# A third gate tile in the stick-breaking list, and bias rows placed behind the gate stores

## The chip, the cores and the metric

The kernel runs on one core of one Trainium2 chip. The metric is the device time of one execution in microseconds (us); lower is better. Engines are named as in the profile: PE (matmul), ACT, DVE, POOL, and SP, which here only issues transfers. POOL issues transfers too.

## The reference

One layer of a hybrid streaming encoder, on a prompt of 1024 rows and a sample of 32 rows, model width 1024. Cut to what matters here:

```python
ada = silu(c) @ w_ada + b_ada            # 6 vectors of 1024: shift1, scale1, gate1, shift2, scale2, gate2
h   = rms_norm(x) * (1 + scale1) + shift1
p   = h @ w_in                           # q/kv latents, rope key, SB q, SB k, SB v, gate A, gate B
z   = einsum('bqhd,bshd->bhqs', q, k) * SB_SCALE            # branch B, stick-breaking, 8 heads
sp  = where(mask, softplus(z), 0)
a   = where(mask, exp(log_sigmoid(z) - (reverse_cumsum(sp) - sp)), 0)
o_B = einsum('bhqs,bshd->bqhd', a, v)
merged = sigmoid(gate_A) * (o_A @ w_proj_a) + sigmoid(gate_B) * (o_B @ w_proj_b)
x   = x + gate1 * rms_norm(merged @ w_out)                  # then the conv FFN
```

## The kernel before, in words

Every fp32 product is made of three matmuls on a high and a low part (`mm3`, L75 to L77). The stages follow one another: normalisation and the first two ada vectors, the q/k/v projection (to about 195 us), the stick-breaking attention (`stage_sb`, about 188 to 505 us), the latents, latent attention, merge, and the FFN.

`stage_sb` runs four passes, one per pair of heads. In each pass `sb_attend` walks a list written by hand, `ORDER`, whose tokens set the order of PE, ACT and DVE exactly. Tokens that matter here:

- `S` scores into a bank, `a e l E` steps on ACT, `x c k d` steps on DVE, `T` transposes (L805), `h v` their split, `V` products with the values, `o p` the output. `p` also stores it (`ob`, L955, on POOL's queue).
- `f` is one k-step (three matmuls) of the gate projection h @ w_in, which fills PE between attention steps. Eight steps make one block of 352 columns in a bank "mm"; there are two such banks.
- `G` empties a finished block: ACT copies the bank into a tile "nat" (L1078), and POOL stores the tile to DRAM (`gd`, L1079). There are two "nat" tiles, used in turn, so a copy waits for the store of the copy before last. PE may start a block only when its bank has been emptied.
- `W` and `w` split the next 128 columns of w_in (raw tile `wr`) into high and low on ACT and DVE.
- `A` multiplies four fetched tiles of w_ada (L240, 32 small matmuls into an "mm" bank), for the ada vectors v = 2 to 5: two `A` tokens in a pass, one vector in a pass. `D` adds the bank to the bias rows on DVE (L246), which frees the bank. For v > 2 the accumulator is one of two "ada" tiles, and `ada_bias` first fills it with the bias, broadcast over 32 partitions: four transfers on POOL's queue (L230).

PE, ACT and DVE obey the list. POOL and SP are placed by a scheduler that may bring a transfer forward when its tile is free. A POOL transfer also waits for the one eight places ahead of it, because eight completion semaphores take turns.

The tiles of `stage_sb` lie in one pool, placed by `place` and the lines around it in a fixed order.

Of the kernel before, what the change touches and what calls it, by code (L numbers as in the profile page):

```python
# [8 lines left out]
F32 = mybir.dt.float32  # L9
F32R = mybir.dt.float32r  # L10
# [7 lines left out]
P = 128  # L18
# [26 lines left out]
class K:  # L45
# [181 lines left out]
    def ada_bias(self, v):  # L227
        for j in range(4):
            c = v * D + j * 256
            self.nc.gpsimd.dma_start(self.acc[32 * j : 32 * j + 32], self.a["b_ada"][0, c : c + 256].partition_broadcast(32))  # L230

    def ada_step(self, n, pool, tp, late):

# [811 lines left out]
    def gates(self):  # L1045

        nc = self.nc
        v = lambda t: t.rearrange("p (k c) -> p k c", k=8)
        w, ps, ada = [self.w_in_tile(2208)], [], []
        self.next_w = w  # L1050
        raw = []

        def steps():
            for m in range(16):
                wh, wl = w.pop(0)
                for b, (c0, n) in enumerate(self.BLK):
                    if b == 0:
                        c = 2208 + (m + 1) * P if m < 15 else 3 * P
                        raw.append(self.wload([(0, 1024, self.a["w_in"][0, :, c : c + P].rearrange("(k p) c -> p k c", p=P), 8)]))
                    ps.append((m, c0, n, self.bank("mm")))  # L1060
                    for k in range(KT):
                        self.mm3(ps[-1][3][:, :n], wh[:, k], wl[:, k], self.Hh[k][:, c0 : c0 + n],
                                 self.Hl[k][:, c0 : c0 + n], k == 0, k == KT - 1)
                        if k < KT - 1:
                            yield
                    if b == 1 and self.ada_sum is not None:
                        ada.append(self.ada_turn())
                    yield

        step = steps()  # L1070

        def do(kind):
            if kind == "f":
                next(step)
            elif kind == "G":
                m, c0, n, x = ps.pop(0)
                g = self.tl(self.At, [P, 512], F32, "nat")
                nc.scalar.copy(g[:, :n], x[:, :n])  # L1078
                nc.gpsimd.dma_start(self.gd[m, :, c0 : c0 + n], g[:, :n])  # L1079
            elif kind == "A":  # L1080
                self.ada_step(4, self.sm2, self.Sp, ada)
                if not self.ada_todo:
                    self.sample_load(1)
            elif kind in "DQ":
                ada.pop(0)()
            elif kind == "W":
                w.append((self.tl(self.W, [P, 1024], F32R, "wh"), self.tl(self.W, [P, 1024], F32R, "wl")))
                self.hi(w[0][0], raw[0])
            else:
                self.lo(w[0][1], raw.pop(0), w[0][0])  # L1090
                w[0] = tuple(v(x) for x in w[0])

        return do
# [14 lines left out]
    def stage_sb(self):  # L1108
        nc = self.nc
        self.att_rows()  # L1110
        S = self.Sp = self.At = self.tc.alloc_tile_pool(name="sb", bufs=2, side="right", reuse_waits="tile")
        def place(*tags):
            for g, w in tags:
                for _ in range(2):
                    self.tl(S, [P, w], F32R if g[0] == "P" else F32, g)

        place(("o", 256), ("PTh", 512), ("PTl", 512))
        self.KLz, Q, KH, V = [None] * 2, [None] * 2, [None] * 2, [None] * 2
        t = lambda n: self.tl(S, [P, TP], F32R, n, 1)

        def values(p, h):
            if p:
                V[h] = t(f"V{h}")
            self.load(V[h].bitcast(F32).rearrange("r (t d) -> r t d", t=8), self.vd[p][:, :, h])

        def queries(p, h):
            r, o = slice(64 * h, 64 * h + 64), slice(64 - 64 * h, 128 - 64 * h)
            d = lambda x, n: self.load(x.bitcast(F32), self.spilt[n][p][r])
            if p:
                Q[h], KH[h] = t(f"Q{h}"), t(f"KH{h}")  # L1130
            d(Q[h][r], "qh")
            d(KH[h][r], "kh")
            d(KH[h][o], "kh")
            d(Q[h][o], "ql")
            d(self.KLz[h][r], "kl")
            d(self.KLz[h][o], "kl")

        V[1], self.KLz[1], Q[1], KH[1] = t("V1"), t("KL1"), t("Q1"), t("KH1")
        place(("ada", 256), ("nat", 512))
        self.diagonals(S)  # L1140
        for _ in range(3):
            self.tl(S, [P, TP], F32, "A")
        V[0], self.KLz[0], Q[0], KH[0] = t("V0"), t("KL0"), t("Q0"), t("KH0")
        self.sm2 = self.tc.alloc_tile_pool(name="att", bufs=2, reuse_waits="tile")
        for g, w, n in (("big", BIG, 3), ("A", TP, 2)):
            for _ in range(n):
                self.tl(self.sm2, [P, w], F32, g)

        self.sent = self.wlast
        queries(0, 0)  # L1150
        self.ada_w, self.ada_sum = [], None
        values(0, 0)

        def score(h, ps, i, c0, n):
            q = slice(i * P, (i + 1) * P)
            nc.tensor.matmul(ps[:, :n], Q[h][:, q], KH[h][:, c0 : c0 + n], start=True, stop=False)
            nc.tensor.matmul(ps[:, :n], Q[h][:, q], self.KLz[h][:, c0 : c0 + n], start=False, stop=True)

        fill = self.gates()
        E = mybir.EngineType  # L1160
        for p in range(4):
            then = {"S2.0a": lambda: queries(p, 1), "S2.1a": lambda: values(p, 1)}
            if p == 0:
                then["S2.1a"] = lambda: (values(p, 1), self.ada_fetch(4, self.sm2))
            if p < 3:
                then.update({"S3.1b": lambda: queries(p + 1, 0), "V3.0": lambda: values(p + 1, 0)})
            with self.tc.manual_schedule(engines={E.PE, E.Activation, E.DVE}):
                self.sb_attend(score, lambda b, h: V[h][:, b * P : b * P + P], self.store(self.obd[p]), fill, then)
        self.in_w.append(self.next_w.pop(0))
        S.release()  # L1170
        self.At = self.sm2
        self.sm3 = self.tc.alloc_tile_pool(name="att2", bufs=2, reuse_waits="tile")
# [1438 lines left out]
```

## Time and profile before

| | |
|---|---|
| median of 3 runs | 1694.51 us (1693.89 to 1695.26) |
| the profiled execution | 1695.23 us, of which the span is 1693.4 us |
| PE busy | 1650.3 us, 97% of the span |
| DVE / ACT / POOL busy | 1268.8 / 995.5 / 296.0 us |
| gate copies (L1078) | 48, the first at 199.2 us, the last at 502.6 us |
| gate stores (L1079) | 48, the first at 208.2 us, the last at 503.4 us |
| bias rows into "ada" (L230) | 12, the first at 201.2 us, the last at 344.0 us |

Timeline rows give: start, duration, engine, line and operation, output<-input, shape, count, and in brackets the idle time of that engine just before it and what ended it. A row of a wait gives: who waited, for whom, us in total, times, longest. Windows give busy time per engine, the TensorE clock that was granted (1.00 is full), the share of DMA engine time, and GB/s.

### The profile page before, as it was taken

The page shows a single profiled execution, that of the slowest core. Times are in us where ns is not written, and L with a number is a line of the kernel's source. Part 1 is how long each engine was busy: PE and PEld are TensorE (multiplying, and loading weights), DVE is VectorE, ACT ScalarE, POOL GpSimd, SP SyncE. Part 2 cuts the span into 40 slices and gives each one's busy share as a digit, 9 for nine tenths or more (in the row PEclk, how much of TensorE's full clock was granted, in tenths as well). Part 3 has the DMA queues.
Part 4 walks back from the last instruction along what each step waited for, and adds up shares of the span by engine and source line. Part 5 has one row for each costly group of instructions (what it writes and reads, how often), then busy time and mean ns, then how long its engine had stood idle before and what let it go on. Part 6 is the DMA issues. An engine that isn't in the chain of part 4 may idle for free. (4 is left out here: it accounts for less than half of the span.)

```text
span 1693.4 us, 30264 instructions
## 1 busy us (share of the span) xinstructions
PE 1650.3 (97%) x11646; PEld 1515.2 (89%) x11646; DVE 1268.8 (75%) x2121; ACT 995.5 (59%) x1945; POOL 296.0 (17%) x569
## 2 busy tenths in 40 slices
PE   5999999999999999999999999999999999999997
PEld 3999989999999898998888799999999999877885
DVE  4865778989883788877766789887787777787456
ACT  4544687878874577776762575444444444554442
POOL 3113312111110311110100222211111111200013
PEclk9999999999999999999999999999999999999999
DMA  9345875566631521221364532433333333697643
GB/s 336 104 133 178 286 232 161 161 190 181 178 116 47 152 65 51 69 82 50 130 228 137 181 115 85 152 105 132 129 102 129 130 104 123 239 323 247 206 141 121
DMA packets 185729, 255.22 MB, mean 151 GB/s; under 512 B 14702, under 2 KB 125056, under 8 KB 185584
## 3 DMA queue, kind: packets, MB, share of 16 engines
q1 hardware_dynamic: 164944, 194.11, 36.8%
q0 software_dynamic: 20416, 59.08, 10.0%
q8 instruction: 92, 1.51, 0.4%
q14 instruction: 53, 0.43, 0.1%
q10 hardware_dynamic: 224, 0.09, 0.0%
HBM read 187.86 MB, written 64.57 MB: 149 GB/s over the span
## 5 line engine op out<-in xcount | busy, mean ns | idle before, releaser
L68 ACT ACTIVATE wh<-wr 128x1024 fp32r<-128x1024 f32 (+5 forms) x163 | 132.1, 819 | 223.7 <-PE s L2065 82.2
L71 DVE TENSOR_TENSOR wl<-wr,wh 128x1024 fp32r<-128x1024 f32 (+5 forms) x163 | 150.2, 929 | 81.2 <-ACT wh L68 81.0
L75 PE MATMUL mm<-hh,wh 128*128 128x352 f32 x456 | 152.9, 335 | 3.7 <-ACT nat L1078 3.7
L76 PE MATMUL mm<-hl,wh 128*128 128x352 f32 x456 | 148.9, 326 | 0.1
L77 PE MATMUL mm<-hh,wl 128*128 128x352 f32 x456 | 148.6, 326 | 0.0
L2064 PE MATMUL mm<-T,wh 128*128 128x256 f32 (+1 forms) x376 | 108.1, 288 | 0.0
L2066 PE MATMUL mm<-T,wl 128*128 128x256 f32 (+1 forms) x376 | 107.1, 285 | 0.4 <-DVE wl L71 0.2
L2065 PE MATMUL mm<-T,wh 128*128 128x256 f32 (+1 forms) x376 | 106.6, 284 | 0.0
L2066 PE MATMUL s<-T,wl 128*128 128x256 f32 (+1 forms) x348 | 99.3, 285 | 0.0
L2064 PE MATMUL s<-T,wh 128*128 128x256 f32 (+1 forms) x348 | 99.2, 285 | 0.0
L2065 PE MATMUL s<-T,wh 128*128 128x256 f32 (+1 forms) x348 | 98.8, 284 | 0.0
L71 DVE TENSOR_TENSOR wl<-S,wh 128x1024 fp32r<-128x1024 f32 (+1 forms) x55 | 59.2, 1078 | 49.7 <-ACT wh L68 49.4
L75 PEld LDWEIGHTS mm<-hh,wh 128*128 128x128 f32 x456 | 86.7, 190 | 7.3 <-ACT nat L1078 3.9
L76 PEld LDWEIGHTS mm<-hl,wh 128*128 128x128 f32 x456 | 86.7, 190 | 2.8 <-issue 0.8
L2205 DVE SCALAR_TENSOR_TENSOR u<-u,c,u 128x1058 f32<-128x1058 f32 x68 | 87.0, 1317 | 2.0 <-ACT u L2202 0.7
L77 PEld LDWEIGHTS mm<-hh,wl 128*128 128x128 f32 x456 | 86.6, 190 | 0.2
L805 PE MATMUL tr<-c,A 128*128 128x128 f32 x576 | 85.0, 272 | 0.3 <-DVE A L921 0.3
L68 ACT ACTIVATE wh<-S 128x1024 fp32r<-128x1024 f32 (+1 forms) x55 | 51.8, 944 | 48.7 <-PE s L2065 13.4
L2064 PE MATMUL tr<-T,wh 128*128 128x272 f32 (+1 forms) x272 | 77.8, 286 | 0.0
L2066 PE MATMUL tr<-T,wl 128*128 128x272 f32 (+1 forms) x272 | 77.7, 286 | 0.0
L2065 PE MATMUL tr<-T,wh 128*128 128x272 f32 (+1 forms) x272 | 77.3, 284 | 0.0
L2195 POOL COPY c<-u 128x2 f32<-128x2 f32 x44 | 26.9, 611 | 265.9 <-DVE u L2141 229.9
(760 smaller groups left out, 5832.8 us busy)
## 6 DMA issues: line engine op xcount, KB each, us to landing
wr<-in_w_up_dram SPq DMA_DIRECT2D x44, 512.0 KB, 4.3
dr<-in_w_down_dram SPq DMA_DIRECT2D x43, 512.0 KB, 5.5
wr<-in_w_in_dram SPq DMA_DIRECT2D x33, 512.0 KB, 6.4
A<-in_w_ada_dram SPq DMA_DIRECT2D x32, 512.0 KB, 5.7
wr<-gdn SPq DMA_DIRECT2D x30, 512.0 KB, 4.2
gdn<-u POOLq DMA_DIRECT2D x23, 512.0 KB, 4.9
gd<-nat POOLq DMA_DIRECT2D x48, 176.0 KB, 3.5
t<-gd SPq DMA_DIRECT2D x16, 528.0 KB, 6.2
```

What stands on the lines that cost most here:

```text
L68: self.nc.scalar.activation(out, in_, AF.Identity, scale=scale)
L71: return self.nc.vector.tensor_tensor(out, full, hi.bitcast(F32), ALU.subtract)
L75: m(ps, lh, rh, start=start, stop=False)
L76: m(ps, lh, rl, start=False, stop=False)
L77: self.pe = m(ps, ll, rh, start=False, stop=stop).ins
L805: self.nc.tensor.transpose(tr[:, (2 * s + q) * P : (2 * s + q + 1) * P], at[q][:, b * P : b * P + P], self.idt)
L2064: m(ps[:, :n], w[0][:, k], x[0][:, k, c], start=first and k == 0, stop=False, skip_group_check=True)
L2065: m(ps[:, :n], w[0][:, k], x[1][:, k, c], start=False, stop=False, skip_group_check=True)
L2066: i = m(ps[:, :n], w[1][:, k], x[0][:, k, c], start=False, stop=k == 3, skip_group_check=True)
L2195: nc.gpsimd.tensor_copy(self.CV[:, 0:2, cc], u[:, 1024:1026])
L2205: nc.vector.scalar_tensor_tensor(y, u[:, w : w + YW], self.cvT[:, w, cc : cc + 1], y, ALU.mult, ALU.add)
```

## The change

Three edits. In the gate step the tile "nat" has three buffers while the list runs in the stick-breaking pool, and two in any other. `ada_bias` issues the rows of v > 2 only after the last gate store that the program has issued so far (`self.gsent`); that is an order on POOL's queue, not a wait for the store to land. `place` takes a count for each tag, so that the third tile has its place; the pool grows by 2 KB per partition, and the tiles placed after "nat" move by that much.

```diff
     def ada_bias(self, v):
         for j in range(4):
             c = v * D + j * 256
-            self.nc.gpsimd.dma_start(self.acc[32 * j : 32 * j + 32], self.a["b_ada"][0, c : c + 256].partition_broadcast(32))
+            with self.tc.issue_after(self.gsent) if v > 2 else ExitStack():
+                self.nc.gpsimd.dma_start(self.acc[32 * j : 32 * j + 32], self.a["b_ada"][0, c : c + 256].partition_broadcast(32))
...
             elif kind == "G":
                 m, c0, n, x = ps.pop(0)
-                g = self.tl(self.At, [P, 512], F32, "nat")
+                g = self.tl(self.At, [P, 512], F32, "nat", 3 if self.At is self.Sp else 2)
                 nc.scalar.copy(g[:, :n], x[:, :n])
-                nc.gpsimd.dma_start(self.gd[m, :, c0 : c0 + n], g[:, :n])
+                self.gsent = nc.gpsimd.dma_start(self.gd[m, :, c0 : c0 + n], g[:, :n]).ins
...
-        place(("o", 256), ("PTh", 512), ("PTl", 512))
+        place(("o", 256, 2), ("PTh", 512, 2), ("PTl", 512, 2))
...
-        place(("ada", 256), ("nat", 512))
+        place(("ada", 256, 2), ("nat", 512, 3))
```

The instructions of PE, ACT, DVE and SP stand in the same order in both programs. Only POOL's queue differs, in where twelve bias rows stand. Lines after L229 are one higher in the changed kernel (L1078 becomes L1079, L230 becomes L231).

POOL, at the start of the list's first pass, before the change. `sbd` is the last spill of the stage ahead, `ada` the bias rows of v = 3 and v = 4, `gd<-nat` the gate stores, `ob` an output store:

```order
L688 DMA sbd<-sb 32x512
L1105 MEMSET ptd_2210 128x128
L1105 MEMSET ptd_2211 128x128
L230 DMA ada_3552<-in_b_ada_dram 32x256 x4
L230 DMA ada_4544<-in_b_ada_dram 32x256 x4
L1079 DMA gd<-nat_2326 128x352
L1079 DMA gd<-nat_2365 128x352
L955 DMA ob_2181<-o_2435 64x256
```

The same place after the change:

```order
L689 DMA sbd<-sb 32x512
L1106 MEMSET ptd_2211 128x128
L1106 MEMSET ptd_2212 128x128
L1080 DMA gd<-nat_2327 128x352
L1080 DMA gd<-nat_2366 128x352
L956 DMA ob_2181<-o_2436 64x256
L1080 DMA gd<-nat_2475 128x352
```

The eight bias rows no longer stand ahead of the first two gate stores.

POOL, in the second pass, after the change; the rows of v = 3 stand here now, between the fourth and fifth gate store of the pass, shortly before the `A` token of the list:

```order
L1080 DMA gd<-nat_3325 128x352
L1080 DMA gd<-nat_3364 128x352
L956 DMA ob_2182<-o_3427 64x256
L1080 DMA gd<-nat_3466 128x352
L1080 DMA gd<-nat_3513 128x352
L231 DMA ada_3553<-in_b_ada_dram 32x256 x4
L956 DMA ob_2182<-o_3609 64x256
L1080 DMA gd<-nat_3622 128x352
```

The rows of v = 4 and v = 5 stand at the same place of the third and fourth pass; before the change those of v = 5 stood in the second pass, behind the store of `o_4041`.

More of the change, by code (lines that the diff above doesn't have):

```diff
@@ L1112, in place @@
         def place(*tags):
-            for g, w in tags:
-                for _ in range(2):
-                    self.tl(S, [P, w], F32R if g[0] == "P" else F32, g)
-        place(("o", 256), ("PTh", 512), ("PTl", 512))
+            for g, w, n in tags:
+                for _ in range(n):
+                    self.tl(S, [P, w], F32R if g[0] == "P" else F32, g, n)
+        place(("o", 256, 2), ("PTh", 512, 2), ("PTl", 512, 2))
         self.KLz, Q, KH, V = [None] * 2, [None] * 2, [None] * 2, [None] * 2
```

## The prediction

> **What bounds the kernel now.** The page's first part says which engine to follow:
>
> ```profile
> PE 1650.3 (97%) x11646; PEld 1515.2 (89%) x11646; DVE 1268.8 (75%) x2121; ACT 995.5 (59%) x1945; POOL 296.0 (17%) x569
> ```
>
> PE is busy 97% of the span, so an edit off PE's path pays only where PE stands still or runs slowly. I therefore read next who made PE wait, after the start-up:
>
> ```profile
> PE mm L75 <- ACT nat L1078: 3.7, 1, 3.7
> PE s L75 <- ACT mh L68: 1.8, 1, 1.8
> ```
>
> The longest stall is one wait for a gate copy, 3.7 us, once; the next is half of it and lies far behind this stage. The timeline of each engine shows where it comes from:
>
> ```profile
> 209.99 0.46 ACT L764 ACTIVATE A<-A 128x320 f32<-128x320 f32 x1
> 215.19 0.45 ACT L1078 COPY nat<-mm 128x352 f32<-128x352 f32 x1 [4.74 <-DMA gd<-nat]
> 215.70 0.43 PE L75 MATMUL mm<-hh,wh 128*128 128x352 f32 x1 [3.65 <-ACT nat L1078]
> 201.20 0.50 POOL L230 DMA_DIRECT2D ada<-in_b_ada_dram  x1 [1.58 <-DMA qh<-T]
> 206.75 1.48 POOL L230 DMA_DIRECT2D ada<-in_b_ada_dram  x3 [0.88 <-DMA ql<-fq]
> 208.22 1.12 POOL L1079 DMA_DIRECT2D gd<-nat  x2
> ```
>
> Read it backwards. PE waits 3.65 us for the third gate copy, which frees its bank. That copy stands 4.74 us on ACT, until the first gate store has landed and its "nat" tile is free. The first store was issued only at 208.22, behind eight bias rows that began at 201.20 and waited in between for spills ahead of them; it landed 215.19 - 208.22 = 7.0 us later.
>
> The windows around it show a second loss, the granted clock:
>
> ```profile
> 212.00:215.70 3.70, 0.05 (x2) 0.00 (x1) 0.37 (x1) 0.51 (x2) 0.00 (x0) 1.00 1.03 384
> 216.70:220.10 3.40, 3.40 (x13) 3.31 (x12) 2.62 (x5) 3.34 (x9) 0.54 (x1) 0.51 1.09 349
> ```
>
> After the stall PE runs 3.40 us at a granted clock of 0.51. What both cost is found without modelling either: the second pass walks the same list, so the same two instructions are taken before and behind the place, in the first pass and in the second:
>
> ```profile
> 205.26 0.49 ACT L744 ACTIVATE A<-s 128x384 f32<-128x384 f32 x1
> 287.26 0.49 ACT L744 ACTIVATE A<-s 128x384 f32<-128x384 f32 x1
> 225.05 0.41 DVE L246 TENSOR_TENSOR acc<-acc,mm 128x256 f32<-128x256 f32 x1
> 301.55 0.41 DVE L246 TENSOR_TENSOR ada<-ada,mm 128x256 f32<-128x256 f32 x1
> ```
>
> 287.26 - 205.26 = 82.00 us ahead of it, 301.55 - 225.05 = 76.50 us behind it. The first pass loses 5.50 us here: 3.65 idle and 1.85 of slow clock and restart.
>
> **The gate stores and the third tile.** Two edits attack the same wait. The third copy gets a tile of its own and waits for no store. The fourth takes the first tile again. Second-pass times less 82.00 give the undisturbed schedule:
>
> ```profile
> 294.93 0.45 ACT L1078 COPY nat<-mm 128x352 f32<-128x352 f32 x1
> L230 POOL DMA_DIRECT2D ada<-in_b_ada_dram x8: 498/498/502, 201.2 to 207.7; - x8
> DMA to landing us min/median/max: 4.9/6.1/6.6
> ```
>
> The fourth copy comes at 294.93 - 82.00 = 212.93. The first store now takes the queue place of the first bias row, 201.20; with the slowest of these landings, 6.6 us, it is in by 207.8, 5 us early. Should it take the 7.0 us measured later, 4.7 us are left. So the stall goes, and -5.50 us is the first term. Its bounds are 0 (something else holds the copy) and -5.50.
>
> **What is late next.** The 5.50 us covered two transfers that do not move with PE, because SP issued them before the stall:
>
> ```profile
> 222.00 1.93 PE L240 MATMUL mm<-A,cT 128*32 128x256 f32 x32
> L83 SPq DMA_DIRECT2D A<-in_w_ada_dram x1: 349/349/349, 206.7 to 206.7; - x1
> DMA to landing us min/median/max: 7.3/7.3/7.3
> 208.77 0.42 SPq L83 DMA_DIRECT2D wr<-in_w_in_dram  x1
> wr<-in_w_in_dram SPq DMA_DIRECT2D x1, 512.0 KB, 11.8
> DMA packets 129, 0.40 MB, mean 398 GB/s; under 512 B 10, under 2 KB 35, under 8 KB 129
> DMA packets 551, 0.33 MB, mean 331 GB/s; under 512 B 10, under 2 KB 536, under 8 KB 551
> 224.32 1.04 ACT L68 ACTIVATE wh<-wr 128x1024 fp32r<-128x1024 f32 x1
> ```
>
> The `A` step moves from 222.00 to 216.50 and needs its fourth w_ada tile after three quarters of 1.93 us, at 217.95. The first tile lands at 206.7 + 7.3 = 214.0, the `wr` load behind all four at 208.77 + 11.8 = 220.6. Spread evenly, the fourth lands at 214.0 + 3/4 x 6.6 = 218.9, a wait of 1.0 us. The packet rows (216 to 217 us, then 217 to 218) say sooner: the short packets of the `wr` load, 512 bytes a row, fill the second row, so the tiles ahead were nearly through by 217, plus about 1.2 us to land: 218.2, a wait of 0.3. It can't be later than the load behind it, 2.65 us, nor less than nothing. I take 0.4, near the packet rows. Then ACT's split of `wr` moves from 224.32 to 218.8 and waits up to 1.8 us for 220.6. What that costs PE is read from the slack behind the same step in the second pass:
>
> ```profile
> 304.63 0.69 DVE L762 TENSOR_TENSOR A<-s,A 128x512 f32<-128x512 f32 x1
> 306.85 0.33 PE L1156 MATMUL s<-KH,Q 128*128 128x384 f32 x1
> ```
>
> DVE frees the score bank at 305.32, PE wants it at 306.85: 1.53 us of slack. Of 1.8 - 0.4 = 1.4 us nothing, of 1.8 us 0.3 comes through; I take 0.1. Both together: +0.5, bounds 0 and 2.7.
>
> **The bias rows.** Twelve rows leave an early place and stand, four each, right behind the last gate store ahead of the `A` token of passes two to four. Nothing is added. POOL's own time is free: behind them stands an output store that waits for DVE anyway, idle 7.47 us. What may cost is that the `D` addition on DVE now waits for rows issued late, and behind it on DVE stands the rest of the list; PE's next gate block waits for the bank that `D` frees.
>
> ```profile
> 295.68 0.54 POOL L1079 DMA_DIRECT2D gd<-nat  x1 [2.02 <-ACT nat L1078]
> DMA to landing us min/median/max: 2.1/2.1/2.1
> 298.00:300.00 2.00, 2.00 (x33) 1.18 (x34) 2.00 (x4) 1.37 (x3) 0.00 (x0) 1.00 0.00 0
> 303.40 0.41 PE L75 MATMUL mm<-hh,wh 128*128 128x352 f32 x1
> 303.69 0.54 POOL L955 DMA_DIRECT2D ob<-o  x1 [7.47 <-DVE o L793]
> L230 POOL DMA_DIRECT2D ada<-in_b_ada_dram x4: 498/501/513, 342.5 to 344.0; - x4
> DMA to landing us min/median/max: 7.2/7.5/7.8
> ```
>
> The rows start at 296.22 and every 0.5 us after, the last at 297.72. The store just ahead landed in 2.1 us, and from 298 to 300 the queues move nothing, so the last row is in by about 299.9, ahead of `D` at 301.55 and of PE's need at 303.40. Cost 0. The far row is the last one: 7.8 us on full queues, landing at 305.5; `D` would wait 4.0 us, of which 303.40 - 301.96 = 1.44 are hidden, so 2.5 us in each of three passes, 7.6 us. I take 0, since the place is quiet.
>
> [...]
>
> **The moved tiles.** The pool's growth moves some waits between instructions. The farthest is a rope-key load in the next stage that now waits for stores of this list:
>
> ```profile
> L1278 SPq DMA_DIRECT2D nat<-in_cache_mla_krope_dram x2: 367/433/499, 539.2 to 539.6; - x2
> L1079 POOL DMA_DIRECT2D gd<-nat x48: 542/571/602, 208.2 to 503.4; - x48
> ```
>
> Some 36 us lie between; cost 0.
>
> **The sum.** -5.5 + 0.5 + 0 = -5.0 us. Against the profiled execution, 1695.23 us (span 1693.4), that gives 1690.2; against the median of 1694.51, which lies 0.7 lower, 1689.5. I take 1689.9. A measurement can tell some 0.2% from no change, 3.4 us, so "faster" begins below 1691.1.
>
> **The rivals.**
>
> *The w_ada tile takes the place of the store.* If the fourth tile lands as late as the load behind it, PE waits 2.65 us at `A` and the gain is 2.8: 1692.4 from the profiled time. For it: the queues are full from 200 to 220 us. Against it: the short packets from 217 on.
>
> *The slow clock isn't in the typical run.* Then the median holds only the 3.65 us of idling and some 0.2 of restart, and the gain is 3.85 - 0.5 = 3.35: 1691.2. For it: the profiled execution is 0.7 us above the median. Against it: the clock fell though PE had already worked 1 us again, so it needs no perfect alignment. [...]
>
> *Late bias rows: slower.* The one place is `D` in passes two to four. If a row needs L us to land, the loss is 3 x (L - 5.27), from 297.72 + L against 301.55 + 1.44. It beats the gain from L = 6.9; at 7.8 the sum is -5.0 + 7.6 = +2.6, 1697.8. For it: rows on full queues needed 7.2 to 7.8. Against it: the quiet window.
>
> *The change doesn't reach the stall*, because the third copy waits for something the trace can't show, such as what lay in the third tile's memory: 1694.5.
>
> **How the numbers follow.** Forecast 0.66, w_ada 0.12, clock 0.11, bias rows 0.06, no effect 0.05. Faster: the forecast and half of the clock case, 0.72. Same: w_ada, the other half, no effect, 0.22. Slower: 0.06. The range starts at the median less the whole 5.5 and 0.3 for the runs' own spread, 1688.7, and ends with the w_ada case, 1692.6; left out are the slow case and no effect.
>
> **What would show it.** Right: no idle before the third gate copy; the first store issued near 201; a granted clock of 1.00 from 212 to 221; the first `D` 5 us earlier; in passes two to four a `D` with no wait for a transfer. Wrong: a PE wait at the `A` step over 2 us, an ACT wait for `wr` that reaches PE, or a DVE wait before L247.

## The result, and the profile after

The changed kernel takes 1690.11 us (median of 22 runs, 1685.59 to 1692.03), the kernel before 1694.02 us (22 runs, 1689.95 to 1696.27). The ratio is 0.9978 with a 95% interval of 0.9972 to 0.9985, so it is 2.5 to 4.7 us faster, 3.7 us at the middle. The profiled execution has a span of 1687.8 us.

The stretch that held the stall, in the same windows as before (busy time of PE, its weight loads, DVE, ACT, POOL; granted clock; DMA share; GB/s):

```profile
PE 1650.3 (98%) x11646; PEld 1514.1 (90%) x11646; DVE 1268.5 (75%) x2121; ACT 995.0 (59%) x1945; POOL 294.9 (17%) x569
212.00:215.70 3.70, 3.70 (x25) 3.67 (x24) 3.44 (x6) 3.57 (x9) 1.11 (x2) 1.00 1.02 406
216.70:220.10 3.40, 3.19 (x40) 1.66 (x39) 3.04 (x7) 2.50 (x5) 0.00 (x0) 1.00 1.09 366
```

From 212.0 to 215.7 PE is busy throughout where it was idle, and from 216.7 the clock is 1.00 where it was 0.51. PE's busy time over the whole span is nevertheless the same to a tenth, 1650.3 us. The reason lies at the start of the program, where this execution ran at half clock for 3.4 us longer than the profiled execution before (first line: before; second: after):

```profile
32.44:35.85 3.41, 3.41 (x17) 1.86 (x17) 3.30 (x5) 2.07 (x4) 0.55 (x1) 0.50 1.05 384
32.46:39.29 6.83, 6.22 (x30) 3.32 (x31) 4.62 (x7) 4.91 (x7) 0.00 (x0) 0.50 1.05 387
```

The timelines of the engines concerned, after the change:

```profile
202.44 0.56 POOL L1080 DMA_DIRECT2D gd<-nat  x1 [1.73 <-ACT A L765]
211.32 0.45 ACT L1079 COPY nat<-mm 128x352 f32<-128x352 f32 x1
219.19 0.64 PE L241 MATMUL mm<-A,cT 128*32 128x256 f32 x8 [0.21 <-DMA A<-in_w_ada_dram]
221.05 1.06 ACT L68 ACTIVATE wh<-wr 128x1024 fp32r<-128x1024 f32 x1 [1.15 <-DMA wr<-in_w_in_dram]
```

The first gate store is issued at 202.44 (the list itself starts 1.0 us later in this execution), the third copy waits for nothing, and the two transfers that were to be late next are: 0.21 us of PE at the fourth w_ada tile, 1.15 us of ACT at the raw w_in tile. The pass offset, taken from the same score step in the first and second pass, and the same step to the first `D`:

```profile
206.23 0.49 ACT L745 ACTIVATE A<-s 128x384 f32<-128x384 f32 x1
220.53 0.41 DVE L247 TENSOR_TENSOR acc<-acc,mm 128x256 f32<-128x256 f32 x1
283.16 0.49 ACT L745 ACTIVATE A<-s 128x384 f32<-128x384 f32 x1
297.44 0.41 DVE L247 TENSOR_TENSOR ada<-ada,mm 128x256 f32<-128x256 f32 x1
```

The step to `D` takes 14.30 us in the first pass and 14.28 in the second; it was 19.79 and 14.29. The offset is 283.16 - 206.23 = 76.93 us, where it was 82.00. So the trace gains 5.07 us in this pass.

The bias rows at their new place in the second pass, with the time from issue to landing:

```profile
L231 POOL DMA_DIRECT2D ada<-in_b_ada_dram x4: 496/501/517, 292.1 to 293.6; - x4
DMA to landing us min/median/max: 2.0/2.1/2.6
```

They land by 293.6 + 2.6 = 296.2, ahead of `D` at 297.44, which shows no wait.

### The profile page after: what moved, and what is told of

Read it like the earlier page. It is cut to its first block, busy times and chain, and to the rows that moved or that the text cites. A ratio compares the mean times of both kernels' runs of the same rounds, so it can differ in the third digit from the quotient of the medians.

```text
span 1687.8 us, 30267 instructions
## 1 busy us (share of the span) xinstructions
PE 1650.3 (98%) x11646; PEld 1514.1 (90%) x11646; DVE 1268.5 (75%) x2121; ACT 995.0 (59%) x1945; POOL 294.9 (17%) x569
```

## The experiments

**Each edit alone.** The theory was that there is one stall and that either edit removes it.

```diff
 # tile only: the changed kernel, less
-            with self.tc.issue_after(self.gsent) if v > 2 else ExitStack():
+            with ExitStack():
```

> The third gate tile alone; the bias rows of v = 3 and v = 4 stay ahead of the first gate stores. Theory (one stall at the third gate copy, and either edit removes it): the third copy doesn't wait; the fourth waits some 2 us for the first store, landed near 215, but PE needs that bank only at the A step, so no PE stall; granted clock 1.00 throughout; some 4 to 5 us faster than before, like the full change. Rival (the queue order is what matters, the tile only helps after it): the wait moves to the fourth copy and PE stalls 1 to 2 us at the A step, so about 2 to 3 us faster only.

Measured: 1690.01 us, ratio to before 0.9974 (0.9963 to 0.9984).

```profile
207.66 1.12 POOL L1080 DMA_DIRECT2D gd<-nat  x2
209.89 0.44 ACT L1079 COPY nat<-mm 128x352 f32<-128x352 f32 x1
214.87 0.45 ACT L1079 COPY nat<-mm 128x352 f32<-128x352 f32 x1 [2.28 <-DMA gd<-nat]
PE mm L241 <- DMA A<-in_w_ada_dram: 1.3, 2, 0.9
204.80 0.49 ACT L745 ACTIVATE A<-s 128x384 f32<-128x384 f32 x1
283.04 0.49 ACT L745 ACTIVATE A<-s 128x384 f32<-128x384 f32 x1
```

The store still goes out behind the bias rows, at 207.66. The third copy has its own tile and doesn't wait; the fourth waits 2.28 us, as both theories had it, and nothing on PE waits for that copy. PE does lose 1.3 us at the `A` step, but to w_ada tiles, which neither theory had named for this kernel. So the wait moved one copy on and stopped being PE's. The pass offset is 283.04 - 204.80 = 78.24 us, 1.3 us above that of the changed kernel.

```diff
 # order only: the changed kernel, less
-                g = self.tl(self.At, [P, 512], F32, "nat", 3 if self.At is self.Sp else 2)
+                g = self.tl(self.At, [P, 512], F32, "nat")
...
-        place(("ada", 256, 2), ("nat", 512, 3))
+        place(("ada", 256, 2), ("nat", 512, 2))
```

> The bias rows behind the gate stores alone, with two gate tiles as before. Theory (either edit is enough): the first store is issued near 201 and lands near 208, ahead of the third copy near 210.5; no ACT wait, no PE stall; 4 to 5 us faster than before. Rival (the store lands later than 210.5 on the full queues, so the tile is needed): an ACT wait of 1 to 3 us is left and a PE stall of up to 2 us; 2 to 4 us faster.

Measured: 1690.36 us, ratio 0.9979 (0.9971 to 0.9988).

```profile
L1080 POOL DMA_DIRECT2D gd<-nat x1: 566/566/566, 201.0 to 201.0; - x1
DMA to landing us min/median/max: 5.7/5.7/5.7
210.26 0.44 ACT L1079 COPY nat<-mm 128x352 f32<-128x352 f32 x1
```

With two tiles the store lands at 201.0 + 5.7 = 206.7 and the third copy finds its tile free at 210.26, 3.5 us later. The rival falls: the queue order needs no third tile. The changed kernel was run again on the same chip:

> The changed kernel once more, on the same chip as its two halves. Theory: 3.5 to 5 us faster than before, the stretch from the 128x384 score step to the first D 14.3 us; the two halves within 1 us of it. Rival (the measured gain of 3.9 us is short of the 5 us because the clock term is missing in typical runs): about 3.4 us.

Measured: 1690.57 us, ratio 0.9976 (0.9967 to 0.9985), which is 2.5 to 5.6 us and holds the rival's 3.4 too. The three medians lie within 0.6 us of each other and their intervals overlap. Either edit alone removes the stall; what the second adds is less than the times can tell. The traces hint that it is not nothing: the pass offset is 78.24 us with the tile alone, 77.02 with the order alone, and 76.48 to 76.93 in three traces of the changed kernel. With the tile alone the bias rows still go out beside the w_ada loads; whether that is why PE waits there, one trace doesn't show.

**What the clock is worth.** PE was kept busy through the stall, with the late copy left as it was.

```diff
 # the kernel before; ORDER, ahead of the gate block that stalls
-... a3.0a h1.1 k2.1a e3.0a d2.1a f4 v1.0 ...
+... a3.0a h1.1 k2.1a e3.0a d2.1a f2 Z f2 v1.0 ...
...
+            elif kind == "Z":
+                if not self.warmed:
+                    self.warmed = True
+                    x = ps[-1][3][:, 352:512]
+                    for _ in range(28):
+                        nc.tensor.matmul(x, self.Hh[0][:, 0:P], self.Hh[1][:, 0:160], start=True, stop=True)
```

> The kernel before, with 28 matmuls of 160 columns, whose result nothing reads, put on PE in the first pass just where it stalls, so that PE is busy for most of the stall while the gate copy is as late as before. Theory (the 1.85 us behind the stall are the granted clock, halved because PE stood idle): granted clock 1.00 after the stall, the pass from the 128x384 score step to the first D takes 17.9 to 18.2 us instead of 19.8, and the kernel is 1.6 to 1.9 us faster than before. Rival (the slow stretch is the restart behind the late copy, whatever PE did): same as before within 0.3 us. If the full change is measured below 5 us because typical runs do not halve the clock, this kernel is not faster either.

Measured: 1692.11 us, ratio 0.9988 (0.9979 to 0.9997).

```profile
211.46 3.25 PE L1090 MATMUL mm<-hh 128*128 128x160 f32 x28
214.09 0.45 ACT L1079 COPY nat<-mm 128x352 f32<-128x352 f32 x1 [4.07 <-DMA gd<-nat]
215.70:220.10 4.40, 4.40 (x40) 3.81 (x42) 3.58 (x8) 4.34 (x11) 0.54 (x1) 1.00 1.04 345
204.84 0.49 ACT L744 ACTIVATE A<-s 128x384 f32<-128x384 f32 x1
284.59 0.49 ACT L744 ACTIVATE A<-s 128x384 f32<-128x384 f32 x1
```

The copy still waits 4.07 us for its store. The 28 matmuls take 3.25 us in its shadow, and behind them the granted clock is 1.00. The pass offset is 79.75 us against 82.00; of those 2.25 us some 0.7 belong to the copy, which here came 9.25 us behind the score step, and 9.93 before. What is left agrees with the 1.6 to 1.9 us expected. The step from the score to the first `D` took 222.65 - 204.84 = 17.81 us, just below the 17.9 to 18.2 expected. Useless work made the kernel faster, by 0.5 to 3.6 us, because idleness cost more than its own length: 5.50 us for 3.65 of idling. The rival (the slow stretch is the restart) is out.

**Whether typical runs halve the clock.** The kernel before was profiled twice more.

> The kernel before, another execution under the profiler. Theory (the halved clock belongs to the stall and is there in most executions): again a stall of 3 to 4 us at the third gate copy and a stretch of 3.4 us at a granted clock near 0.5 behind it; 19 to 20 us from the 128x384 score step to the first D. [...]

> As the other look at the kernel before: theory, a halved clock again, 19 to 20 us from the 128x384 score step to the first D; rival, a clock of 1.00 and some 18 us in one of the looks.

The second and the third trace, the stretch of half clock in each, and the ends of the pass offset:

```profile
215.63 0.66 PE L75 MATMUL mm<-hh,wh 128*128 128x352 f32 x1 [4.20 <-ACT nat L1078]
214.90:221.70 6.80, 6.07 (x21) 5.99 (x22) 3.97 (x8) 5.44 (x12) 1.11 (x2) 0.50 0.93 317
204.65 0.49 ACT L744 ACTIVATE A<-s 128x384 f32<-128x384 f32 x1
288.36 0.49 ACT L744 ACTIVATE A<-s 128x384 f32<-128x384 f32 x1
```

```profile
217.39 0.43 PE L75 MATMUL mm<-hh,wh 128*128 128x352 f32 x1 [3.46 <-ACT nat L1078]
218.40:221.80 3.40, 3.40 (x13) 3.32 (x12) 2.62 (x5) 3.34 (x9) 0.54 (x1) 0.50 1.09 347
207.15 0.49 ACT L744 ACTIVATE A<-s 128x384 f32<-128x384 f32 x1
288.93 0.49 ACT L744 ACTIVATE A<-s 128x384 f32<-128x384 f32 x1
```

Three executions in three halve the clock, one of them for twice as long. Their pass offsets are 82.00, 83.71 and 81.78 us, so the stall costs 5.3 to 7.2 us against the undisturbed 76.5. Behind this stall, in these three traces, the slow stretch was always there and only its length differed: 3.4, 6.8 and 3.4 us.

**Late bias rows on purpose.** This is the mechanism of the slower rival, made to happen.

```diff
 # the changed kernel, ahead of the rows in ada_bias
+        if v > 2:
+            with self.tc.issue_after(self.gsent):
+                for _ in range(8):
+                    self.gsent = self.nc.gpsimd.memset(self.acc, 0.0).ins
```

> The changed kernel with eight POOL memsets of the ada tile ahead of each set of bias rows of v > 2 (the rows overwrite them), so that the rows start about 3 us later, behind the start of the next w_ada loads. Theory (a D addition that waits costs PE only what goes beyond 1.4 us of slack): rows land 4 to 6 us after their start, D in passes two to four waits 3 to 5 us, PE loses 1.5 to 3.5 us in each pass, 5 to 10 us in all against the changed kernel, so slower than it and 0 to 6 us slower than before. Rival (late rows are free: nothing that PE needs stands behind D): as fast as the changed kernel, some 4 us faster than before.

Measured: 1707.03 us, ratio 1.0081 (1.0067 to 1.0094), some 17 us above the changed kernel.

```profile
295.24 1.99 POOL L235 DMA_DIRECT2D ada<-in_b_ada_dram  x4 [0.29 <-POOL ada L231]
303.38 0.42 DVE L251 TENSOR_TENSOR ada<-ada,mm 128x256 f32<-128x256 f32 x1 [5.92 <-DMA ada<-in_b_ada_dram]
303.85 0.66 PE L75 MATMUL mm<-hh,wh 128*128 128x352 f32 x1 [4.38 <-DVE ada L251]
302.88:309.71 6.83, 5.86 (x20) 5.86 (x21) 6.30 (x10) 0.83 (x2) 1.09 (x2) 0.50 1.07 224
388.22:391.63 3.41, 3.41 (x14) 3.41 (x13) 3.38 (x7) 0.79 (x2) 1.09 (x2) 0.50 1.05 237
470.14:473.55 3.41, 3.41 (x14) 3.41 (x13) 3.38 (x7) 0.81 (x2) 1.09 (x2) 0.50 0.31 73
PE mm L75 <- DVE ada L251: 12.1, 3, 4.4
```

The direction was right and the size too small. `D` waits 5.92 us and PE 4.38, so 1.54 us are hidden, close to the 1.44 of the prediction. But with each stall the granted clock fell to 0.50, for 6.83, 3.41 and 3.41 us. The three stalls sum to 12.1 us. PE is busy for 12.7 us of the slow stretches, which at 0.50 costs it some 6.3 us more by estimate, 18.4 in all, near the 17 between the medians. The expectation had left the clock out. The rival, that late rows are free, is out.

**The next wait in line.** In the first pass the w_ada fetch was put ahead of the load of the second head's values.

```diff
-                then["S2.1a"] = lambda: (values(p, 1), self.ada_fetch(4, self.sm2))
+                then["S2.1a"] = lambda: (self.ada_fetch(4, self.sm2), values(p, 1))
```

> The changed kernel with the first four w_ada tiles fetched ahead of the values of the second head in the first pass. Theory (what is late next is the fourth w_ada tile, 0 to 0.5 us, then the raw w_in tile on ACT): no PE wait at the first A step, the pass offset 76.45 us, 0 to 0.4 us faster than the changed kernel, which the times cannot tell, only the trace. Rival (the values are wanted sooner than the second pass shows): a PE wait at the first product of the second head, slower by up to 2 us.

Measured: 1687.95 us, ratio 0.9967 (0.9955 to 0.998), which would be 2 us better than the changed kernel. But the two had not run side by side, so both were run once more on one chip:

> The early w_ada fetch beside the changed kernel on one chip. Theory (it removes 0 to 1.3 us of waiting for w_ada tiles, most where an execution reaches the list early): no PE wait at the first A step, pass offset 76.5 us, and a median 0 to 1 us below the changed kernel, inside the intervals. Rival (the 2 us between the two in their separate runs are real): 2 us below the changed kernel again, ratio to before near 0.9967.

> The changed kernel a third time, as the partner of the early fetch. Theory: 3.5 to 5 us faster than before, a PE wait of 0 to 0.5 us at the first A step. Rival: as the early fetch says, 2 us slower than it.

Measured: 1691.26 us, ratio 0.9975 (0.9966 to 0.9984), beside 1690.23 us, ratio 0.9973 (0.9963 to 0.9983) for the changed kernel. The 2 us did not come back. In both traces of the early fetch PE had no wait at the `A` step. But the raw w_in tile was late on ACT, by 0.68 us in the first trace, where PE waited for nothing, and by 2.33 in the second:

```profile
223.79 1.06 ACT L68 ACTIVATE wh<-wr 128x1024 fp32r<-128x1024 f32 x1 [2.33 <-DMA wr<-in_w_in_dram]
207.80 0.49 ACT L745 ACTIVATE A<-s 128x384 f32<-128x384 f32 x1
285.48 0.49 ACT L745 ACTIVATE A<-s 128x384 f32<-128x384 f32 x1
```

The offset is 77.68 us in the second trace, 1.2 above the undisturbed one, and 76.48 in the first. A reading that fits is that on full queues one transfer moved ahead moves another back; these two traces don't show it. None of the versions here beats the changed kernel beyond its noise.

## Why the prediction was right

*The stall goes (-5.5).* Right: the third copy no longer waits, PE is busy through the old gap, and the step to `D` fell by 5.49 us. It also goes with either edit alone. The prediction had said that both edits attack the same wait, but priced them only together.

*The slow clock belongs to the stall.* Right, and shown: filling the stall with useless matmuls keeps the clock at 1.00. The rival by which the typical run has no slow clock, at 0.11, has three traces against it. What taking this slow clock away is worth in the whole run is another matter (see the sum).

*What is late next (+0.5).* Right in kind and size: 0.21 us at the fourth w_ada tile and 1.15 us of ACT at the raw tile; the offset of 76.93 is 0.43 above the undisturbed 76.50. The 1.2 us to landing in that step stood without a row; in the trace of the kernel before, 98% of the short packets of the `wr` load had ended by 219.4 and the load landed at 220.5, so it is of the right size. The wait depends on the execution: PE waited for no w_ada tile in two more traces of the changed kernel, and 1.3 us with the third tile alone. With the order alone and in the second early fetch the late raw tile reached PE, by 0.3 and 0.6 us. The rival at 2.65 us is an upper end that no trace came near.

*The bias rows (0).* Right, but with little room: the rows landed in 2.0 to 2.6 us in the second pass, and no `D` of the changed kernel waits for one. In the third pass, which the prediction did not price apart, the last row took 3.3 to 3.8 us in its three traces and landed 0.55 to 0.13 us ahead of `D`; with the order alone `D` waited 0.15 us. The price of the slower rival was sized by waiting alone; when it was made to happen, the slack came out as argued (1.54 against 1.44) and the clock made it dearer.

*The moved tiles (0).* No wait for the rope-key load shows in PE's list after the list of this stage.

*The sum.* The pass gained 5.07 us where 5.0 was forecast. The times gained less: 3.7 us by the ratio, 2.5 to 4.7 by its interval, 3.9 to 4.6 us by the medians of the three comparisons of the changed kernel. That 1689.9 lies so near 1690.11 is in part luck. It started from a median of 1694.51, 0.5 above that of the 22 runs, and took 4.6 off it where the medians differ by 3.9; the two errors nearly cancel.

The step that is too large is the one that took the gain of one stretch for the gain of the run, as if all else stayed. The averages over three traces of each kernel show what happened instead. The first pass gains 5.9 us (an offset of 76.6 against 82.5), more than forecast. But the list begins 0.9 us later (at 206.6 against 205.7), and from the score step of the second pass to the end the kernel before takes 1403.9 to 1406.1 us, the changed one 1404.6 to 1407.1, on average 1.2 us more. That leaves 3.8 us, which is what the times show.

Both losses go with slow clock. In two of the three traces of the changed kernel a stretch behind the list ran at half clock (second and third line; the fourth is the same work in the first trace):

```profile
521.54:524.95 3.41, 2.84 (x23) 2.53 (x22) 0.97 (x4) 0.95 (x2) 0.57 (x1) 1.00 0.02 5
524.95:528.36 3.41, 3.41 (x15) 3.41 (x15) 0.49 (x3) 1.17 (x2) 0.54 (x1) 0.50 0.03 7
525.29:528.70 3.41, 3.41 (x15) 3.41 (x14) 0.18 (x1) 1.17 (x2) 0.54 (x1) 0.50 0.03 7
524.90:528.30 3.40, 3.40 (x25) 3.40 (x24) 0.43 (x3) 1.07 (x2) 0.54 (x1) 1.00 0.05 12
```

Each costs PE some 1.7 us, an estimate from 3.41 us at 0.50; no trace of the kernel before has one there. The clock that is on record for every run points the same way. One minus the clock, times the span, is an estimate of what slow clock costs a run. On the chip of the two halves it falls from 10.9 us (28 runs before) to 9.8 (10 runs after), and on the chip of the last comparison from 11.2 (18 runs) to 10.8 (8 runs), where the slow clock and restart of the stall were priced at 1.85. So the term that came out too large is the slow clock's, by some 0.7 to 1.4 us: it leaves the stall, and part of it turns up elsewhere. Whether the change brings this about or it is chance stays open; three traces a side are few, and the fill, which keeps the old order, has the later slow stretch too.

The start of the list varies ahead of any edit: the score step of the first pass comes between 204.31 and 207.80 us in the twelve traces. That goes with the slow clock at the start of the program. Five traces with 6.8 us of it there begin between 204.31 and 205.26, two with 10.2 us at 205.17 and 206.23, five with 13.7 us between 206.61 and 207.80. Both programs show short and long ones, the kernel before 6.8, 6.8 and 13.7, the changed one 10.2, 13.7 and 13.7.

## What to carry to other kernels

Where a schedule repeats, compare the same two instructions in a disturbed and an undisturbed pass: the difference prices a stall with everything it drags along, here 5.5 us where the wait itself showed 3.65. Then compare the rest of the run too: what a stretch gains, the run need not gain. Look behind a long stall of PE for a slow granted clock, and count it; here 3.65 us of waiting cost half as much again. A stall that is a buffer waiting for its store can be mended at either end, one more buffer or an earlier place in the store's queue, and one of the two may be enough. Ask what was loading in its shadow: here it was late next.

## What the runs showed of the hardware

Three things stand out. In the first trace of the kernel before the clock was at 0.51 from 216.7 us on, though PE had already been working again from 215.70. And the slow clock outlasted the restart: in the second trace of that kernel PE worked from 215.63 on, and the clock stayed at 0.50 until 221.7, 6.1 us later.

The third is that behind the same work the clock was halved in some executions (0.50 in the second trace of the changed kernel) and not in others (1.00 in the first). The slow stretches of all traces between the start and the end of the program last 3.41, 6.83, 10.24 or 13.65 us, one to four steps of 3.413 (13.65 / 4). The full-clock stretches between them are whole steps too (484.69 us, 142 of them, in the second trace of the changed kernel; 180.91 us, 53 of them, in the first trace of the kernel before), so the changes of the clock can be laid on a grid. Behind the list, near 524 us in the changed kernel, PE runs small matmuls (64 columns) with a gap between them and then transposes, 4.4 us together at full clock. This is the gap in the second trace of the changed kernel:

```profile
523.41 1.08 PE L978 MATMUL pv<-A,big 128*128 128x64 f32 x8 [0.57 <-DVE A L981]
```

In four of the twelve traces a whole step of the grid, counted on from the last change of the clock, falls inside that work, and in these four the next step runs at half clock. In the other eight no whole step does, and the clock stays at 1.00. In the second trace of the changed kernel that step is 521.54 to 524.95, and PE stood idle for only 0.57 us of it. This is a pattern in twelve traces; no run moved the work along the grid on purpose.
